# Weight and token sums issued ahead of their use, an output projection over eight banks, and transposes moved to other pairs

## The chip, the cores and the metric

The kernel runs on one core of a Trainium2 chip. That core has five engines, each with its own instruction queue that is worked off in order: TensorE (PE, matrix products), VectorE (DVE), ScalarE (ACT), GpSimd (POOL) and SyncE (SP, here the queue that issues the loads of weights). The metric is the device time of one execution in microseconds (us); the median of several executions is compared.

## The reference

One layer of a decoder trunk on 16 learned meta tokens and 256 tokens, width 2048, everything in float32. Three blocks add to the residual stream h:

```python
u = rms_norm(h, ffn1_norm_g[l])
h = h + 0.5 * swiglu(u, ffn1_w_gate[l], ffn1_w_up[l], ffn1_w_down[l])
...
z = u @ w_in[l]
q, k, v, qi, ki, wi, xc, gate_b, gate_c, ga, gc = jnp.split(z, SPLIT_POINTS, axis=-1)
...
merged = jax.nn.sigmoid(ga) * y_attn + jax.nn.sigmoid(gc) * y_conv
h = h + merged @ w_out[l]
...
h = h + 0.5 * swiglu(u, ffn2_w_gate[l], ffn2_w_up[l], ffn2_w_down[l])
return h[:, N_META:]
```

The change touches the second half: the two gates (ga and gc, each 2048 wide), the output projection w_out (2048 by 2048), and the second FFN (2048 to 5632 and back). The first FFN, the attention with its choice of 64 keys, and the short convolution stay as they are.

## The kernel before, in words

**Products in two parts.** A float32 product is made of three products of a faster 32-bit format: every operand is split into a high part (ACT copies it into that format) and a low part (DVE subtracts the copy from the original). High by high, high by low and low by high are added up in a PSUM bank. Weights are streamed, so each weight must be split when it comes: the class `Stream` does that.

**The stream.** A load (`load`, L126) brings 1 MB (128 x 2048) into one of three raw buffers, four in the second FFN. A load is cut into steps (`subs`) of at most 128 x 1024. `split` (L154) makes the high part (L175, tile `whi`) on ACT and the low part (L176, tile `wlo`) on DVE; there are four split buffers, six in the second FFN. Each time TensorE's program comes to a new step, `next` (L199) does, in this order: what was put down with `early`, the split of the step that lies three ahead (five in the second FFN), what was put down with `later` and is due, and then hands out the blocks. The lag given to `later` counts such calls: 1 is the next one. Since all engines take their instructions in the order in which they were written down, these calls set the order on ACT, DVE and POOL.

**Seven products instead of eight.** In the gates and the second FFN the work goes in groups. A group makes two blocks of 256 tokens by 512 columns (gate and up, or two column blocks of the down product) over pairs of 128 rows of the weights; a pair is one load. A pair of kind C takes the eight plain products (`plain_half`, twice, with a `hook(n)` between the halves). A pair of kind S takes seven products of sums, in Strassen's manner: sums of tokens (`sums_into`, L578, four subtractions and additions on POOL) against sums of weights. The weight sums are three DVE additions: `sumsa` (L143) and two for `sumsb` (L150, L151). An S load has four steps: "one" (128 x 512, raw), "sa" and "sb" (the sums) and "two" (raw). `total` writes down the additions of sa directly before the split of sa, and those of sb directly before the split of sb. The S pairs add into the banks q1, q5, q6, q7 besides q2 and q3 and q4, the C pairs into q2, q3, q4, q8. After the last S pair of a group `recombine` (L626) reads q1, q5, q6 and q7 into SBUF, which frees them; at the group's end `after_end` adds the rest.

**Order of the kinds.** In the gates, and in the first group of the second FFN, the order is `FIRST`, CCSCSCCC. In the other groups it is `KINDS`, SCCSCCCC; the last down group, with six pairs, has SCCCCC.

**Turns.** A gate column and an FFN group come out with tokens on the partitions; for the next product they are transposed on TensorE into two banks and split from there (`turn_four`, L596, with the copies at lags 1 and 2). `turn_merged` does it for the gates' result, `turn_mid` for the FFN's intermediate: for a group in the next up group at pair 5, for the last group of a part in the first half of the down group, at pair 5 of 8 or 3 of 6. The residual h is transposed in the first group of the second FFN (`turn_h`, eight turns, three banks, three to a pair from pair 5).

**Token sums.** `sums_of_tokens` (L586) scales two rows of h on ACT, sums on POOL, splits on ACT and DVE, all written down at once: for the gates twice, ahead of the first gate column (L1077), and for the second FFN inside the output projection (`made_of`, L1145).

**Output projection.** 16 tiles of 128 rows, each over 16 blocks (L1149 to L1163). The last four blocks come from the last gate column, which is still to be transposed, so four tiles take their first 12 blocks side by side in banks q2, q3, q4, q8, with loads of 12 and then of 4 blocks; the other 12 tiles follow in the same four banks by turns. After a tile, `add_to` (L375: DVE, ACT, DVE) adds it to h, and one call later `next_act2` and `square` make the next operands.

Of the kernel before, what the change touches and what calls it, by code (L numbers as in the profile page):

```python
# [9 lines left out]
F32 = mybir.dt.float32  # L10
# [5 lines left out]
P = 128  # L16
# [35 lines left out]
WIDE = 512  # L52
NG = FF // WIDE
PAIRS = KD // 2
KINDS = "SCCSCCCC"
ORDER = [2, 0, 1, 4, 3, 5, 6, 7]
PARTS = [range(0, 4), range(4, 8), range(8, NG)]
PLAN = [step for gs in PARTS for step in [("up", g) for g in gs] + [("down", gs)]]


FIRST = "CCSCSCCC"


def pairs_up(g):
# [16 lines left out]
class Stream:  # L81
# [7 lines left out]
    def __init__(self, nc, raw_pool, split_pool):  # L89
        self.nc = nc  # L90
        self.raw_pools, self.raw_bufs, self.n_raw = [raw_pool], RAW_BUFS, 0
        self.split_pools, self.ahead, self.n_tiles = [split_pool], AHEAD, 0
        self.sum_pool = None
        self.loads, self.subs = [], []
        self.raw, self.ready, self.sums = {}, {}, {}
        self.n_loaded = self.n_split = self.at = 0
        self.blocks, self.waiting, self.steps = [], [], []
        self.first = []
# [34 lines left out]
            self.raw[self.n_loaded] = raw  # L133
            self.n_loaded += 1

    def total(self, g, kind):

        raw = self.raw[g]
        name = f"sum{kind}"
        to = self.sum_pool.tile([P, 2 * WIDE], F32, name=name, tag=name)  # L140
        self.sums[g, kind] = to
        if kind == "sa":
            self.nc.vector.tensor_add(  # L143
                to.rearrange("p (q c) -> p q c", q=2),
                raw[:, WIDE : 3 * WIDE].rearrange("p (q c) -> p q c", q=2),
                raw[:, 3 * WIDE :].rearrange("p (q c) -> p q c", q=1).to_broadcast([P, 2, WIDE]),
            )
        else:
            sa = self.sums.pop((g, "sa"))
            self.nc.vector.tensor_add(to[:, :WIDE], sa[:, WIDE:], raw[:, WIDE : 2 * WIDE])  # L150
            self.nc.vector.tensor_add(to[:, WIDE:], to[:, :WIDE], raw[:, :WIDE])  # L151
        return to

    def split(self, upto):  # L154
        nc = self.nc
        while self.n_split < min(upto, len(self.subs)):
            if self.subs[self.n_split][1] == "sa" and not self.sum_pool:
                return
            g, kind, c, kk, width = self.subs[self.n_split]
            self.load(g + self.raw_bufs)  # L160
            n = kk * width
            if kind in ("sa", "sb"):
                raw = self.total(g, kind)
            elif kind == "two":
                raw = self.raw[g].rearrange("p (q c) -> p q c", c=WIDE)[:, 0:3:2, :]
            else:
                raw = self.raw[g][:, c : c + n]
            pool = self.split_pools[self.n_tiles % len(self.split_pools)]
            self.n_tiles += 1
            hi = pool.tile([P, SUB], F32R, name="whi")  # L170
            lo = pool.tile([P, SUB], F32R, name="wlo")
            to = [x[:, :n] for x in (hi, lo)]
            if kind == "two":
                to = [x.rearrange("p (q c) -> p q c", q=2) for x in to]
            nc.scalar.activation(to[0], raw, AF.Copy)  # L175
            nc.vector.tensor_sub(to[1], raw, to[0].bitcast(F32))  # L176
            self.ready[self.n_split] = [
                (hi[:, i * width : (i + 1) * width], lo[:, i * width : (i + 1) * width]) for i in range(kk)
            ]
            self.n_split += 1  # L180
            if kind == "sb":
                del self.sums[g, kind]
            if self.n_split == len(self.subs) or self.subs[self.n_split][0] > g:
                self.load(g + 1 + self.raw_bufs)

# [45 lines left out]
def tile_decoder_layer(  # L231
# [34 lines left out]
    def chunks(src, i0, i1, width=P):  # L266
        for i in range(i0, i1):
            st.add(src[i], RAW // width, width)
# [18 lines left out]
        for i in range(KC // 2):  # L287
            st.add(wb[c * KC // 2 + i], 4, WIDE)
    for a, b in ((0, 12), (12, KD)):
        for d in range(4):  # L290
            st.add(wo[d, :, a * P : b * P], b - a, P)
    chunks(wo, 4, KD)
    i = 0
    for kind, at in PLAN:
        for k in [p[0] for p in (pairs_up(at) if kind == "up" else pairs_down(at) * 2)]:
# [88 lines left out]
    def split_into(hi, lo, src):  # L384
        nc.scalar.activation(hi, src, AF.Copy)
        nc.vector.tensor_sub(lo, src, hi.bitcast(F32))
# [191 lines left out]
    def sums_into(t, x):  # L578

        t = t.rearrange("p (f t) -> p f t", f=4)  # L580
        nc.gpsimd.tensor_sub(t[:, 0, :], x[:, 0, :P], x[:, 0, P:])
        nc.gpsimd.tensor_sub(t[:, 1, :], x[:, 0, P:], x[:, 1, P:])
        nc.gpsimd.tensor_add(t[:, 2, :], x[:, 1, P:], t[:, 0, :])
        nc.gpsimd.tensor_sub(t[:, 3, :], x[:, 1, :P], t[:, 2, :])

    def sums_of_tokens(i, gain, to):  # L586

        x = small_tile("m0").rearrange("p (j t) -> p j t", j=2)
        t = small_tile("m1")
        for j in range(2):  # L590
            d = 2 * i + j
            nc.scalar.activation(x[:, j, :], h[:, d, META:], AF.Copy, scale=gain[:, d : d + 1])
        sums_into(t, x)
        split_into(to[:, 0, :], to[:, 1, :], t)

    def turn_four(to, m, tags, extra=None):  # L596

        for j in range(NT):
            ps = bank(tags[j], "pt")
            for f in range(4):  # L600
                nc.tensor.transpose(ps[:, f * P : (f + 1) * P], m[j][:, f * P : (f + 1) * P], ident)

            def after(j=j, ps=ps):
                cols = slice(j * P, (j + 1) * P)
                src = ps.rearrange("p (f t) -> p f t", f=4)
                for a, b, x in to:
                    split_into(x[:, :, 0, cols], x[:, :, 1, cols], src[:, a:b, :])
                if extra:
                    extra(src, cols)

            st.later(after, 1 + j)

    def group(todo, hook, after_seven, after_end):

# [36 lines left out]
    with ExitStack() as mix:  # L651
# [422 lines left out]

        act1 = act[:, :, :, LATER + META : LATER + T]
        made1 = {i: gp.tile([P, 2, 4 * P], F32R, name=f"made{i}") for i, k in enumerate(FIRST) if k == "S"}
        for i, to in made1.items():  # L1077
            sums_of_tokens(i, gains[1], to)

        ms, merged = {}, []  # L1080
        places = [[("tA", 4)], [("tB", 4)], [("zz0", 2), ("zz1", 2)], [("c0", 4)]]
# [64 lines left out]
            made[i] = spare[:, len(made)]  # L1146
            sums_of_tokens(i, gains[2], made[i])

        po = [bank(tag, "po") for tag in ("q2", "q3", "q4", "q8")]  # L1149
        for d in range(4):  # L1150
            paired(po[d], lambda k: ms[k], 0, 12, KD)
            if d == 1:
                turn_merged(("q1", "q5"))
        for d in range(KD):
            if d < 4:
                paired(po[d], lambda k: ms[k], 12, KD, KD)
            else:
                po.append(bank(("q2", "q3", "q4", "q8")[d % 4], "po"))
                paired(po[d], lambda k: ms[k], 0, KD, KD)
            st.later(lambda d=d: add_to(h[:, d, META:], po[d], 1.0, True))  # L1160
            st.later(lambda d=d: (next_act2(d), square(d, META)), 2)
            if d % 2 and FIRST[d // 2] == "S":
                st.later(lambda d=d: made_of(d // 2), 3)  # L1163
# [60 lines left out]
    def up_group(g):  # L1224

        def hook(n):
            if g == 0:
                if n == 0:
                    st.later(lambda: nc.vector.tensor_add(ssq[0][:, META:], ssq[0][:, META:], ssq[1][:, META:]))
                if n == 5:  # L1230
                    norm2()
                if n >= 5:
                    for i in range(3 * n - 15, min(3 * n - 12, 8)):
                        turn_h(i // 2, i % 2, ("q7", "q6", "q5")[i % 3])
            elif n == 5:
                turn_mid(("q1", "q5"))

        def after_end(q, buf):
            for tag in ("q3", "q2", "q4", "q8"):
                nc.vector.tensor_add(buf[tag], q[tag][0], buf[tag])  # L1240
            for j, tag in enumerate(("q2", "q3")):
                nc.scalar.activation(buf[tag], buf[tag], AF.Silu, scale=r2[:, 2 * j : 2 * j + 1])

            def products():
                m = [small_tile(f"m{j}") for j in range(NT)]
                for j, (u, s) in enumerate((("q4", "q2"), ("q8", "q3"))):
                    nc.vector.scalar_tensor_tensor(
                        m[j], buf[u], r2[:, 2 * j : 2 * j + 1], buf[s], op0=ALU.mult, op1=ALU.mult
                    )
                waiting.append((g, m))  # L1250

            st.later(products, 2)

        group(
            [(k, lambda i=i: four_of(act2, 2 * i, 2 * i + 1), lambda i=i: made[i]) for k, i in pairs_up(g)],
            hook, lambda buf: None, after_end,
        )

    PLACES = {"q2": (0, 0), "q3": (1, 0), "q4": (0, 1), "q8": (1, 1)}

    def down_group(gs, final):
        pairs = pairs_down(gs)
        for half in range(2):
# [13 lines left out]
            def after_end(q, buf, place=place):  # L1277
# [8 lines left out]
                    (k, lambda g=g, f=f: four_of(mids[g], f, f + 1), lambda g=g, f=f: made_mid[g, f])  # L1286
                    for k, g, f in pairs
                ],
                lambda n: n == len(pairs) - 3 and half == 0 and turn_mid(("q1", "q5")), after_seven, after_end,
            )  # L1290

    right = []
# [142 lines left out]
```

## Time and profile before

| | us |
|---|---|
| median of 3 runs | 2184.57 (2184.21 to 2185.79) |
| profiled execution, its own time | 2186.47 |
| span of the profiled execution, first to last instruction | 2184.7 |
| TensorE busy | 2149.4 |
| DVE busy | 1456.2 |
| ACT busy | 1035.0 |
| POOL busy | 60.4 |
| mean granted clock of TensorE | 0.997 |

Busy time is the time in which an engine had an instruction of the program at work. TensorE's pipelined matmuls overlap a little, and their ends are modelled. The view of waits gives, for an engine and a line, what it waited for in total, how often, and the longest. A timeline row gives the start, the time taken, the engine, the line, the operation with the tile written and the tiles read, the count, and in brackets the idle time before it and what ended that.

The stages in the profile: first FFN to about 800 us, projections, attention and convolution to 1086, the gates in four columns to 1353, the output projection to 1446, the second FFN to the end at 2184.7, with its down groups beginning near 1632, 1894 and 2112.

### The profile page before, as it was taken

Reading aid. Unit: us, or ns where it says so; the run is one execution under the profiler, and the core shown is the slowest. Engines: PE = TensorE matmul, PEld = TensorE weight load, DVE = VectorE, ACT = ScalarE, POOL = GpSimd, SP = SyncE. Lnnn points to the kernel's source line nnn. Section 1 sums busy time; section 2 is a strip of 40 time slices with the busy share of each in tenths; the row PEclk is TensorE's granted clock in tenths of the full one; section 3 lists DMA queues with packets and bytes.
Section 4 is the critical chain, followed back from the end, with each engine's and each line's share of the span. In section 5 each row is a group of like instructions: output and inputs, shape, how many; then the busy total and the mean of one; then the engine's idle time right before and its main releaser. Section 6 shows DMA issues by size and latency. Waiting matters only on the chain.

```text
span 2184.7 us, 31757 instructions
## 1 busy us (share of the span) xinstructions
PE 2149.4 (98%) x13102; PEld 1929.8 (88%) x13102; DVE 1456.2 (67%) x1823; ACT 1035.0 (47%) x1343; POOL 60.4 (3%) x82
## 2 busy tenths in 40 slices
PE   8999999999999999999999999999999999999998
PEld 8999999999999998898978888877887888878887
DVE  7555544455555555786567766678787878877785
ACT  6444433344444445564454444556554545444552
POOL 3000000000000000000000000110000000000000
PEclk9999999999999999999999999999999999999999
DMA  6555555555555545444455454555545554555453
GB/s 246 192 176 182 183 174 175 179 183 178 174 177 183 181 167 173 157 158 149 155 192 193 176 190 169 198 193 193 193 178 188 212 192 176 190 202 202 174 195 132
DMA packets 56881, 397.69 MB, mean 182 GB/s; under 512 B 6336, under 2 KB 6464, under 8 KB 9760
## 3 DMA queue, kind: packets, MB, share of 16 engines
q1 hardware_dynamic: 56448, 395.08, 50.9%
q8 instruction: 102, 1.67, 0.3%
q0 software_dynamic: 144, 0.42, 0.1%
q14 instruction: 43, 0.35, 0.0%
q10 hardware_dynamic: 144, 0.17, 0.0%
HBM read 393.54 MB, written 2.10 MB: 181 GB/s over the span
## 4 chain that ended last, share of the span: by engine, by line
PE 86%; DVE 8%; ACT 3%; issue 1%; POOL 1%; DMA 0%; SPq 0%; ACTq 0%; DVEq 0%
PE q L558 11%; PE q L557 11%; PE q L556 11%; DVE wlo L176 4%; PE pd L351 4%; PE pd L350 4%; PE pd L352 4%; PE pu L350 4%; PE pg L350 4%; PE pg L352 4%; PE pu L352 4%; PE pg L351 4%; PE pu L351 4%; ACT whi L175 3%; PE po L365 1%
## 5 line engine op out<-in xcount | busy, mean ns | idle before, releaser
L176 DVE TENSOR_TENSOR wlo<-raw,whi 128x1024 fp32r<-128x1024 f32 (+1 forms) x751 | 875.9, 1187 | 558.2 <-ACT whi L175 552.4
L175 ACT ACTIVATE whi<-raw 128x1024 fp32r<-128x1024 f32 (+1 forms) x751 | 757.7, 1026 | 752.8 <-PE q L558 146.1
L556 PE MATMUL q<-whi,act 128*128 128x512 f32 x898 | 352.0, 392 | 3.6 <-ACT u L381 2.3
L557 PE MATMUL q<-wlo,act 128*128 128x512 f32 x898 | 350.5, 390 | 2.3 <-DVE wlo L176 2.3
L558 PE MATMUL q<-whi,act 128*128 128x512 f32 x898 | 350.1, 390 | 0.0
L556 PEld LDWEIGHTS q<-whi,act 128*128 128x128 f32 x898 | 169.0, 188 | 39.9 <-ACT u L381 2.7
L557 PEld LDWEIGHTS q<-wlo,act 128*128 128x128 f32 x898 | 169.0, 188 | 37.9 <-DVE wlo L176 3.5
L350 PE MATMUL pd<-mid,whi 128*128 128x272 f32 x704 | 201.7, 286 | 0.0
L351 PE MATMUL pd<-mid,whi 128*128 128x272 f32 x704 | 201.7, 286 | 0.0
L352 PE MATMUL pd<-mid,wlo 128*128 128x272 f32 x704 | 201.7, 286 | 0.0
L558 PEld LDWEIGHTS q<-whi,act 128*128 128x128 f32 x898 | 169.0, 188 | 35.4
L350 PE MATMUL pg<-act,whi 128*128 128x272 f32 x672 | 192.7, 287 | 0.0
L352 PE MATMUL pg<-act,wlo 128*128 128x272 f32 x672 | 192.5, 287 | 0.0
L351 PE MATMUL pg<-act,whi 128*128 128x272 f32 x672 | 192.5, 287 | 0.0
L350 PE MATMUL pu<-act,whi 128*128 128x272 f32 x672 | 192.5, 286 | 0.0
L351 PE MATMUL pu<-act,whi 128*128 128x272 f32 x672 | 192.5, 286 | 0.0
L352 PE MATMUL pu<-act,wlo 128*128 128x272 f32 x672 | 192.5, 286 | 0.0
L350 PEld LDWEIGHTS pd<-mid,whi 128*128 128x128 f32 x704 | 132.6, 188 | 0.0
L351 PEld LDWEIGHTS pd<-mid,whi 128*128 128x128 f32 x704 | 132.6, 188 | 0.0
L352 PEld LDWEIGHTS pd<-mid,wlo 128*128 128x128 f32 x704 | 132.6, 188 | 0.0
L351 PEld LDWEIGHTS pg<-act,whi 128*128 128x128 f32 x672 | 126.6, 188 | 0.0
L350 PEld LDWEIGHTS pg<-act,whi 128*128 128x128 f32 x672 | 126.6, 188 | 0.0
(281 smaller groups left out, 3591.9 us busy)
## 6 DMA issues: line engine op xcount, KB each, us to landing
raw<-in_w_dram SPq DMA_DIRECT2D x132, 1024.0 KB, 4.9
raw<-in_wgu_dram SPq DMA_DIRECT2D x87, 1024.0 KB, 4.8
raw<-in_wd_dram SPq DMA_DIRECT2D x44, 1024.0 KB, 4.7
raw<-in_wg_dram SPq DMA_DIRECT2D x32, 1024.0 KB, 4.9
raw<-in_wcv_dram SPq DMA_DIRECT2D x24, 1024.0 KB, 4.8
raw<-in_wb_dram SPq DMA_DIRECT2D x16, 1024.0 KB, 4.9
raw<-in_wo_dram SPq DMA_DIRECT2D x12, 1024.0 KB, 4.9
raw<-in_wqi_dram SPq DMA_DIRECT2D x8, 1024.0 KB, 4.8
```

The costliest lines, as they stand in the source:

```text
L175: nc.scalar.activation(to[0], raw, AF.Copy)
L176: nc.vector.tensor_sub(to[1], raw, to[0].bitcast(F32))
L350: nc.tensor.matmul(ps, whi, xhi, start=first, stop=False)
L351: nc.tensor.matmul(ps, whi, xlo, start=False, stop=False)
L352: nc.tensor.matmul(ps, wlo, xhi, start=False, stop=last)
L365: nc.tensor.matmul(ps.rearrange("p (a t) -> p a t", a=2), whi, x(i), start=i == 0, stop=False)
L556: nc.tensor.matmul(ps, xhi, whi, start=n == 0, stop=False)
L557: nc.tensor.matmul(ps, xhi, wlo, start=False, stop=False)
L558: nc.tensor.matmul(ps, xlo, whi, start=False, stop=n == total - 1)
```

## The change: what it does

- `total` goes. `sum_ahead` writes down all three additions of an S load before the split of the step ahead of its first one ("one"), together with the load that this allows.
- `sums_of_tokens` puts its three parts down with `later`: scaling and POOL sums at lag `at` + 1, the split at lag `at` + 3. The gates' two calls are set three calls apart.
- `turn_four` puts both copies down at lag 1.
- `KINDS` becomes SCSCCCCC, with the order of the pairs to match. `turn_mid` comes one pair sooner in all places; the turns of h and the norm come one pair later, at pairs 6 (three turns) and 7 (five turns, over four banks).
- In the output projection five tiles stand side by side instead of four, and the tiles go through all eight banks; the turn of the last gate column uses q6 and q7 instead of q1 and q5.

```diff
-KINDS = "SCCSCCCC"
-ORDER = [2, 0, 1, 4, 3, 5, 6, 7]
+KINDS = "SCSCCCCC"
+ORDER = [2, 0, 4, 1, 3, 5, 6, 7]
...
+SIDE = 5
...
+    def sum_ahead(self):
+
+        for g, kind, _, _, _ in self.subs[self.n_split : self.n_split + 2]:
+            if kind in ("one", "sa") and self.sum_pool and g not in self.summed:
+                self.load(g + self.raw_bufs)
+                self.summed.add(g)
+                raw = self.raw[g]
+                sa, sb = (self.sum_pool.tile([P, 2 * WIDE], F32, name=f"s{i}", tag=f"s{i}") for i in "ab")
+                self.nc.vector.tensor_add(
+                    sa.rearrange("p (q c) -> p q c", q=2),
+                    raw[:, WIDE : 3 * WIDE].rearrange("p (q c) -> p q c", q=2),
+                    raw[:, 3 * WIDE :].rearrange("p (q c) -> p q c", q=1).to_broadcast([P, 2, WIDE]),
+                )
+                self.nc.vector.tensor_add(sb[:, :WIDE], sa[:, WIDE:], raw[:, WIDE : 2 * WIDE])
+                self.nc.vector.tensor_add(sb[:, WIDE:], sb[:, :WIDE], raw[:, :WIDE])
+                self.sums[g, "sa"], self.sums[g, "sb"] = sa, sb
...
                 return
+            self.sum_ahead()
             g, kind, c, kk, width = self.subs[self.n_split]
...
             if kind in ("sa", "sb"):
-                raw = self.total(g, kind)
+                raw = self.sums.pop((g, kind))
...
     for a, b in ((0, 12), (12, KD)):
-        for d in range(4):
+        for d in range(SIDE):
             st.add(wo[d, :, a * P : b * P], b - a, P)
-    chunks(wo, 4, KD)
+    chunks(wo, SIDE, KD)
...
-    def sums_of_tokens(i, gain, to):
+    def sums_of_tokens(i, gain, to, at=0):
...
-        for j in range(2):
+
+        def scaled(j):
             d = 2 * i + j
             nc.scalar.activation(x[:, j, :], h[:, d, META:], AF.Copy, scale=gain[:, d : d + 1])
-        sums_into(t, x)
-        split_into(to[:, 0, :], to[:, 1, :], t)
+
+        st.later(lambda: [scaled(j) for j in range(2)], at + 1)
+        st.later(lambda: sums_into(t, x), at + 1)
+        st.later(lambda: split_into(to[:, 0, :], to[:, 1, :], t), at + 3)
...
-            st.later(after, 1 + j)
+            st.later(after)
...
-        for i, to in made1.items():
-            sums_of_tokens(i, gains[1], to)
+        for n, (i, to) in enumerate(made1.items()):
+            sums_of_tokens(i, gains[1], to, 3 * n)
...
-        po = [bank(tag, "po") for tag in ("q2", "q3", "q4", "q8")]
-        for d in range(4):
+        tags = ("q2", "q3", "q4", "q8", "q1", "q5", "q6", "q7")
+        po = [bank(tags[d], "po") for d in range(SIDE)]
+        for d in range(SIDE):
             paired(po[d], lambda k: ms[k], 0, 12, KD)
             if d == 1:
-                turn_merged(("q1", "q5"))
+                turn_merged(("q6", "q7"))
         for d in range(KD):
-            if d < 4:
+            if d < SIDE:
                 paired(po[d], lambda k: ms[k], 12, KD, KD)
             else:
-                po.append(bank(("q2", "q3", "q4", "q8")[d % 4], "po"))
+                po.append(bank(tags[d % 8], "po"))
...
-                if n == 5:
+                if n == 6:
                     norm2()
-                if n >= 5:
-                    for i in range(3 * n - 15, min(3 * n - 12, 8)):
-                        turn_h(i // 2, i % 2, ("q7", "q6", "q5")[i % 3])
-            elif n == 5:
+                if n >= 6:
+                    for i in range(3) if n == 6 else range(3, 8):
+                        turn_h(i // 2, i % 2, ("q7", "q6", "q5", "q1")[(i - n + 6) % 4 if n > 6 else i])
+            elif n == 4:
                 turn_mid(("q1", "q5"))
...
-                lambda n: n == len(pairs) - 3 and half == 0 and turn_mid(("q1", "q5")), after_seven, after_end,
+                lambda n: n == len(pairs) - 4 and half == 0 and turn_mid(("q1", "q5")), after_seven, after_end,
```

More of the change, by code (lines that the diff above doesn't have):

```diff
@@ L94, in __init__ @@
         self.loads, self.subs = [], []
-        self.raw, self.ready, self.sums = {}, {}, {}
+        self.raw, self.ready, self.sums, self.summed = {}, {}, {}, set()
         self.n_loaded = self.n_split = self.at = 0
@@ L134, in load @@
             self.n_loaded += 1
[L136 to L152, printed above, removed]
+    def sum_ahead(self):
[13 more added lines that the diff above has]
+                self.sums[g, "sa"], self.sums[g, "sb"] = sa, sb
     def split(self, upto):
@@ L180, in split @@
             self.n_split += 1
-            if kind == "sb":
-                del self.sums[g, kind]
             if self.n_split == len(self.subs) or self.subs[self.n_split][0] > g:
```

## The prediction, made before the changed kernel was run

> **What bounds the kernel now.** I read the first lines of the page, then the waits of TensorE alone, then the same view in the stretch of each stage, and last the timelines of ScalarE (ACT) and VectorE (DVE) in front of each wait.
>
> ```profile
> span 2184.7 us, 31757 instructions
> PE 2149.4 (98%) x13102; PEld 1929.8 (88%) x13102; DVE 1456.2 (67%) x1823; ACT 1035.0 (47%) x1343; POOL 60.4 (3%) x82
> ...
> PE q L556 <- ACT mid L385: 5.9, 3, 2.3
> PE q L557 <- DVE wlo L176: 5.2, 9, 0.8
> PE q L556 <- ACT u L381: 2.3, 1, 2.3
> PE q L556 <- ACT whi L175: 2.3, 3, 1.0
> PE pht L1221 <- DVE vx L631: 2.3, 1, 2.3
> PE q L558 <- DVE mid L386: 1.4, 3, 0.6
> PE po L365 <- ACT whi L175: 1.4, 3, 0.9
> PE po L365 <- ACT u L381: 0.4, 1, 0.4
> PE pht L1221 <- DVE ve L633: 0.2, 1, 0.2
> ```
>
> Columns of the waits: us in total, times, longest. TensorE is busy for all but 35 us, and the change takes no matmul away. So it can win only these waits, which sum to 21.4 us, and what they cost in clock. By stage:
>
> ```profile
> PE q L557 <- DVE wlo L176: 2.7, 4, 0.8
> PE q L556 <- ACT whi L175: 2.1, 2, 1.0
> ...
> PE q L557 <- DVE wlo L176: 1.0, 3, 0.3
> ...
> PE q L557 <- DVE wlo L176: 1.5, 2, 0.8
> ```
>
> The stretches are the start of the gates (1085 to 1150), the other gates (1150 to 1350) and the entry to the second FFN (1446 to 1490). That places the 21.4: A, start of the gates 4.8; B, three later gate columns 1.0; C, output projection 1.8 (the two po rows); D, entry 4.0 (2.3 for u, 1.5, and 2.3 - 2.1 = 0.2 for whi); E, transposes of h 2.5 (the pht rows); F, the three down groups 7.3 (the mid rows).
>
> The clock costs more:
>
> ```profile
> 1485.00:1488.40 3.40, 3.40 (x11) 2.73 (x10) 2.51 (x4) 1.67 (x4) 0.00 (x0) 0.50 0.70 212
> 1488.40:1491.80 3.40, 3.40 (x16) 2.80 (x16) 0.99 (x1) 1.06 (x1) 0.00 (x0) 0.99 0.40 166
> 1669.30:1672.70 3.40, 3.40 (x10) 2.62 (x9) 0.73 (x2) 1.06 (x1) 0.00 (x0) 0.51 0.00 0
> 1928.75:1935.55 6.80, 6.28 (x14) 4.50 (x15) 3.50 (x5) 1.37 (x2) 0.00 (x0) 0.50 0.08 34
> ```
>
> The figure after the POOL column is the granted clock. It is half in three stretches, 13.6 us together, each right behind a wait of 2.3 us: E's, and F's first and second. Half clock costs at most 13.6 / 2 = 6.8. By the counts (16 matmuls in 3.4 us at full clock, so 5, 6 and 18 are missing, at 0.21 us, less 0.5 idle) it costs 5.7. I take 6.2: E 1.6, F 4.6. The third F wait, and D's 2.3 us, were followed by none.
>
> **A and B: sums ahead.** A weight tile of kind S needs 1215 + 683 + 714 ns = 2.6 us of sums, then low halves of 1224 ns:
>
> ```profile
> L143 DVE TENSOR_TENSOR sumsa<-raw 128x1024 f32<-128x1024 f32 x40 | 48.6, 1215 | 0.0
> L151 DVE TENSOR_TENSOR sumsb<-sumsb,raw 128x512 f32<-128x512 f32 x40 | 28.5, 714 | 1.4
> L150 DVE TENSOR_TENSOR sumsb<-sumsa,raw 128x512 f32<-128x512 f32 x40 | 27.3, 683 | 0.0
> L176 DVE TENSOR_TENSOR wlo<-raw,whi 128x1024 fp32r<-128x1024 f32 x699 | 842.5, 1224 | 543.1 <-ACT whi L175 541.2 <-PE po L365 0.5 <-PE q L558 0.5
> 1094.40 1.56 ACT L175 ACTIVATE whi<-raw 128x1024 fp32r<-128x1024 f32 x2
> 1098.53 1.06 ACT L175 ACTIVATE whi<-sumsa 128x1024 fp32r<-128x1024 f32 x1 [2.57 <-DVE sumsa L143]
> 1446.25 0.40 PE L556 MATMUL q<-whi,act 128*128 128x512 f32 x1
> 1449.45 0.39 PE L558 MATMUL q<-whi,act 128*128 128x512 f32 x1
> ```
>
> The last two rows are the first and last of 15 matmuls: 3.20 / 14 = 0.229 us each. So a half pair of kind C (12 matmuls) is 2.74 us, an S pair (21) 4.80. ACT waits 2.57 for a sum, while DVE idles 541 us in all ahead of low halves, for ACT. At the start of the gates all token sums, with a round trip over POOL, also stand before the first weight split at 1094.40. Now that split comes first, and the sums fill DVE's idle time. The same three additions run, none is saved.
>
> What they pass is the low half of the C half pair in front. Count from TensorE's start of a later gate column (0). DVE first has six operations of the merge, 6 x 0.68 = 4.1; sums to 6.7, that low half to 7.9; its matmul comes at 3 x 2.74 + 0.23 = 8.4. The second S: with four buffers the first S's last step can't be split before TensorE has left four half pairs, 10.9; split 1.06, two low halves 2.4: 14.4; sums 17.0, low half 18.2; its matmul comes at 4 x 2.74 + 4.80 + 2.74 + 0.23 = 18.7. Spare 0.5 each time. The same count with the old order has the second S's third low half at 23.8 against 23.5, a wait of 0.3, which is the row 1.0 over 3. In the first column DVE has one token split more (0.69), so 0.2 may stay. A wins 4.6, B 1.0. Both ends: if the spare is missed by its own size, 8 x 0.5 = 4 us come back; none can win more than its wait. The next load, now issued before the buffer's last reader, waits on SP for that reader as before; behind it on SP stand only later loads.
>
> In the second FFN six buffers run five steps ahead. At a group's start DVE does four additions (2.7), sums (2.6) and a low half (1.2), done at 6.5 against 4.80 + 2.74 + 0.23 = 7.8: nothing lost, 1.3 spare. S pairs at places 0 and 2 instead of 0 and 3 leave one C pair between them, which that count includes. That cover gone, an S pair costs up to its 2.6.
>
> **C: output projection.** Before, tile 4 waited for bank q2 (0.4); with eight banks no tile waits. The stall then goes to the backlog of additions behind the side-by-side tiles:
>
> ```profile
> 1374.91 1.23 DVE L176 TENSOR_TENSOR wlo<-raw,whi 128x1024 fp32r<-128x1024 f32 x1 [3.03 <-ACT whi L175]
> 1377.86 1.22 DVE L176 TENSOR_TENSOR wlo<-raw,whi 128x1024 fp32r<-128x1024 f32 x1 [0.52 <-ACT whi L175]
> 1381.22 1.23 DVE L176 TENSOR_TENSOR wlo<-raw,whi 128x1024 fp32r<-128x1024 f32 x1 [0.52 <-ACT whi L175]
> 1388.53 1.23 DVE L176 TENSOR_TENSOR wlo<-raw,whi 128x1024 fp32r<-128x1024 f32 x1 [0.52 <-ACT whi L175]
> 1393.41 1.23 DVE L176 TENSOR_TENSOR wlo<-raw,whi 128x1024 fp32r<-128x1024 f32 x1 [0.53 <-ACT whi L175]
> 1376.93 2.11 PE L365 MATMUL po<-ms,whi 128*128 128x512 f32 x8 [0.37 <-ACT u L381]
> ```
>
> A half tile is 8 matmuls of 512 columns and 8 of 256, 12 x 0.229 = 2.75 us. In the backlog DVE needs 3.4 a half tile (1377.86 to 1381.22), then 7.3 for two; afterwards 4.9 a whole tile (1388.53 to 1393.41) against 5.5. Before, DVE entered it 2.0 us ahead of TensorE (1374.91 against 1376.93). Five tiles side by side mean one addition more, one small load more on SP, one split more on ACT and DVE. The next tile's 1 MB load waits for the third load ahead of it, and between the two now lies a step of 1.4 where one of 2.75 lay: 1.4 later, so DVE enters 0.6 ahead. High halves are then ready at 2.8, 6.2, 10.1 and 13.8 (3.4, 3.9 and 3.7 apart), wanted at 2.75, 5.6, 9.0 and 12.9: 0.1 + 0.6 + 1.1 + 0.9 = 2.7 us. Against this the two waits behind the token sums go:
>
> ```profile
> 1400.55 1.32 POOL L581 TENSOR_TENSOR vm<-vm 128x128 f32<-128x128 f32 x1 [5.30 <-ACT vm L592]
> 1402.79 0.46 POOL L584 TENSOR_TENSOR vm<-vm,vm 128x128 f32<-128x128 f32 x1
> 1403.95 0.69 DVE L386 TENSOR_TENSOR act<-vm,act 128x512 fp32r<-128x512 f32 x1 [2.40 <-ACT act L385]
> ```
>
> DVE idled 2.40 there, twice; the split now comes two half tiles after the POOL work. Behind that on POOL stand only sums of squares, wanted in the next stage. POOL's four operations took 2.7, the first 1.32 while DVE worked, the last 0.46. Low end: no backlog stall, 0. High end: all four take 1.3, so 5.3, and 2.0 us of new waits. I take 2.7 for the projection, 0.9 worse than now. [...]
>
> **D: entry.**
>
> ```profile
> 1453.53 0.42 DVE L413 TENSOR_TENSOR ssq<-ssq,sq 128x256 f32<-128x256 f32 x1
> ```
>
> The last projection tile sat in q8, needed by the first pair: 2.3 us. Now the last four sit in q1, q5, q6, q7, which the first S needs 11 us later: gone. But DVE is free only at 1453.95, 7.7 after TensorE's start at 1446.25; sums and low half then end at 7.7 + 2.6 + 1.2 = 11.5, and the fourth half pair wants them at 8.4: a new wait of 3.0 in the place of the old. If DVE comes 4.8 earlier (both 2.40 stalls gone) it is nil. I take 1.8; the two S waits (1.5) and 0.2 go. D wins 2.2, so C and D together 1.3.
>
> **E and F: turns on other pairs.**
>
> ```profile
> 1482.56 0.69 DVE L631 TENSOR_TENSOR vx<-q,vv 128x512 f32<-128x512 f32 x1
> 1665.65 1.06 ACT L175 ACTIVATE whi<-sumsa 128x1024 fp32r<-128x1024 f32 x1 [3.99 <-DVE sumsa L143]
> 1666.62 0.58 ACT L385 ACTIVATE mid<-pt 128x512 fp32r<-128x512 f32 x1
> ```
>
> E: the turns wanted banks that DVE freed at 1483. One pair later is 5.5 us later: 2.5 and the clock's 1.6 won. Five turns now fall into one hook with four banks; the fifth waits for an ACT copy issued behind one split, 1.06 + 0.59 against 16 transposes, 1.8: about nil, 0.5 at most. F: the second copy (1666.62) stood behind a split that waited 3.99 for a sum. Now there is no such wait, both copies come in one step, and the turn comes one pair (5.5 us) sooner, against a lateness of 2.3 + 0.6. The tightest is the last down group, counted on DVE from its start: 4 additions 2.7, 4 low halves 4.9, 2 products 1.5, 4 recombinations 2.7, so bank q5 is free at 11.8, and the turn comes at 4.80 + 3 x 2.74 = 13.0; 4 additions 2.7, 4 low halves 4.9, 2 copies 1.4: 20.8, wanted at 4.80 + 6 x 2.74 = 21.2. F wins 7.3 and 4.6 of clock; low end: half a microsecond late three times.
>
> **The sum.** 4.6 + 1.0 + 1.3 + 2.5 + 7.3 + 6.2 = 22.9. The profiled execution took 2186.47, its span 2184.70 with 1.77 around it; 2163.6 of it is left. It lies 0.09% over the median of 2184.57, from which I count: 2161.7. Own range 2157 (all 27.6 won) to 2166.
>
> **Rivals.**
> 1. The projection and its handover lose more: POOL at 1.3 an operation (2.0), DVE as late at the entry as now (1.2), and a half-clock stretch behind that 3 us wait (1.6): 2166.5. For it: 1.32; against: DVE has idle time between its operations (0.52 before each row above).
> 2. The turns of F still come late, because DVE's queue (the last count leaves 0.4) reaches the copies late: F gives 4 of its 11.9, 2169.6; with rival 1 2174.
> 3. The clock drops don't hang on these waits. D's 2.3 us was followed by none. Then 6.2 stays: 2167.9. Against it: three drops, three waits directly ahead. [...] The rows show drops behind 2.3.
> 4. Slower: the sums in front of a low half, on DVE's queue, make it late at each of 40 S pairs. It decides from where DVE reaches the sums over 0.5 us (8 in the gates) or 1.3 us (32 in the FFN) later than counted. 2.0 us late costs 8 x 1.5 + 32 x 0.7 = 34.4: 2196.1. For it: the small spare; against: the 541 us of DVE's idle time ahead of low halves, where the sums go.
> 5. All waits gone: 2157.
>
> **Chances.** Forecast 0.52, rival 1 0.20, 2 0.10, 3 0.08, 4 0.05, 5 0.05. Under 0.2% (4.4 us) this kernel's time can't be told from no change. Faster: all but rival 4 and a part (0.04) of 2 that grows past 2180: 0.91. Same 0.05, slower 0.04. Range 2156.5 to 2174, up to rivals 1 and 2 together.
>
> **What would show it.** Right: ACT no longer waits for a weight sum; the rows q on mid, u and both pht rows are gone; granted clock 1.00 from 1480 to 1940. C: waits po on whi of 2 to 3 us, behind tile 5. D: one wait q on wlo at the fourth half pair. Wrong: new waits q on wlo at every S pair (rival 4), mid rows left over (2), half clock without a wait (3).

## The result and the profile after

The changed kernel takes 2159.32 us (median of four, 2158.81 to 2160.26), the kernel before beside it 2185.18 (2184.21 to 2187.13): 0.9881 of the time, 95% interval 0.9864 to 0.9898. The forecast was 2161.7, range 2156.5 to 2174. The profiled execution took 2160.26.

First lines of the page after, then TensorE's waits (us in total, times, longest):

```profile
span 2158.5 us, 31730 instructions
PE 2140.2 (99%) x13102; PEld 1929.4 (89%) x13102; DVE 1462.1 (68%) x1824; ACT 1043.2 (48%) x1344; POOL 72.6 (3%) x82
...
PE q L556 <- DVE wlo L177: 3.1, 2, 2.8
...
PE po L364 <- ACT whi L176: 1.4, 2, 0.7
```

The nine rows of before that the change could reach, 21.4 us in 25 waits, have become these two: 4.5 us in four. (The other rows, such as those of the first FFN, belong to stages that nothing was changed in.) Gone are both rows on `mid`, both on `pht`, and both of ACT's u. By the prediction's letters: A and B keep 0.3 us, C 1.4, E and F nothing. D has one wait of 2.8, at the fourth half pair as foretold, longer than foretold.

What ACT waited for, before (first two rows) and after (last two):

```profile
ACT whi L175 <- DVE sumsa L143: 100.2, 29, 4.3
ACT whi L175 <- DVE sumsb L151: 91.1, 36, 3.6
```

```profile
ACT whi L176 <- DVE sa L145: 9.2, 7, 1.7
...
ACT whi L176 <- DVE sb L150: 5.5, 3, 2.1
```

191 us of waiting for weight sums became 15. DVE's work is about the same (1462 us busy against 1456): the sums only stand elsewhere in its queue.

Windows behind two of the old waits on `mid` before, then the whole stretch from 1480 to 1940 after; the figure behind the POOL column is the granted clock, and it is 1.00 throughout:

```profile
1660.00:1680.00 20.00, 17.07 (x71) 13.22 (x70) 12.34 (x14) 5.84 (x7) 0.00 (x0) 0.91 0.36 130
1920.00:1945.00 25.00, 22.56 (x89) 17.58 (x88) 16.61 (x21) 8.59 (x10) 0.00 (x0) 0.86 0.34 127
```

```profile
1480.00:1940.00 460.00, 460.00 (x2072) 381.68 (x2072) 379.74 (x422) 246.38 (x281) 16.09 (x16) 1.00 0.55 196
```

And the new wait at D, in DVE's timeline (start, us, operation, in brackets the idle time before) and in two windows:

```profile
1446.33 0.42 DVE L412 TENSOR_TENSOR ssq<-ssq,sq 128x256 f32<-128x256 f32 x1
1446.66 1.22 DVE L145 TENSOR_TENSOR sa<-raw 128x1024 f32<-128x1024 f32 x1
...
1449.25 1.82 DVE L177 TENSOR_TENSOR wlo<-raw,whi 128x1024 fp32r<-128x1024 f32 x2
...
1447.30:1450.71 3.41, 0.59 (x2) 0.28 (x3) 3.34 (x5) 2.77 (x4) 0.00 (x0) 1.00 0.00 0
1450.71:1454.13 3.42, 3.42 (x9) 2.67 (x9) 3.42 (x5) 1.61 (x2) 0.00 (x0) 0.50 0.80 249
```

The second FFN began at 1438.80. DVE works off the tail of the projection until 1446.66, 7.9 us later, then does the three sums, and only at 1449.25 begins the low half that TensorE wants at 1447.7. The wait is followed by 3.4 us of half clock: 9 matmuls, where windows of this length at full clock held 16 or 17 (under the last heading). This execution has one more stretch of half clock, in the first FFN, that the change doesn't touch: 17.12 to 20.53, with 18 matmuls where the kernel before has 30 in as much time. The execution reaches the gates 1.1 us later (1087.24 against 1086.11). The sums below leave this stretch out unless they name it.

### The profile page after: what moved, and what is told of

Same layout as the page of the kernel before. It is cut to its first block, busy times and chain, and to the rows that moved or that the text cites. A ratio compares the mean times of both kernels' runs of the same rounds, so it can differ in the third digit from the quotient of the medians.

```text
span 2158.5 us, 31730 instructions
## 1 busy us (share of the span) xinstructions
PE 2140.2 (99%) x13102; PEld 1929.4 (89%) x13102; DVE 1462.1 (68%) x1824; ACT 1043.2 (48%) x1344; POOL 72.6 (3%) x82
## 4 chain that ended last, share of the span: by engine, by line
PE 94%; DVE 3%; ACT 2%; issue 1%; POOL 0%; DMA 0%; SPq 0%; ACTq 0%
PE q L556 13%; PE q L557 13%; PE q L555 13%; PE pd L351 4%; PE pd L350 4%; PE pd L349 4%; PE pu L349 4%; PE pg L349 4%; PE pu L350 4%; PE pg L350 4%; PE pg L351 4%; PE pu L351 4%; DVE wlo L177 1%; PE pbr L557 1%; PE pbr L555 1%; PE pbr L556 1%
## 5 line engine op out<-in xcount | busy, mean ns | idle before, releaser
L176 ACT ACTIVATE whi<-raw 128x1024 fp32r<-128x1024 f32 (+1 forms) x752 | 766.6, 1027 | 863.6 <-PE q L557 240.2
L350 PEld LDWEIGHTS pg<-act,whi 128*128 128x128 f32 x672 | 126.6, 188 | 0.0
L349 PEld LDWEIGHTS pu<-act,whi 128*128 128x128 f32 x672 | 126.6, 188 | 0.0
```

What stands on the lines that cost most here:

```text
L349: nc.tensor.matmul(ps, whi, xhi, start=first, stop=False)
L350: nc.tensor.matmul(ps, whi, xlo, start=False, stop=False)
```

## The experiments

Each figure is the median of four executions or more, taken beside the kernel before:

| kernel | us |
|---|---|
| before (its medians beside the experiments) | 2185.4 to 2186.6 |
| changed | 2159.3 |
| changed, weight sums in steps | 2185.6 |
| the same, and second S pair at its old place | 2195.0 |
| changed, turns of `mid` and S place as before | 2164.2 |
| the same, and second copy one step later | 2168.5 |
| changed, turns of h as before | 2159.3 |
| changed, token sums at once | 2167.0 |
| changed, second S pair at its old place | 2166.7 |
| changed, four tiles side by side | 2157.3 |
| four tiles, first sums of FFN2 later | 2155.3 |
| four tiles, first S pair of FFN2 later | 2153.8 |
| before, with the weight sums ahead alone | 2171.4 |
| before, with the early turn of `mid` alone | 2205.7 |

**Weight sums in steps.**

```diff
-            self.sum_ahead()
...
-                raw = self.sums.pop((g, kind))
+                raw = self.total(g, kind)
```

> The changed kernel with the weight sums of a kind S tile written where they stood before, each just ahead of the high half that reads it. My theory (each stage's waits went with the part of the change that I named for it): the start of the gates and the later gate columns lose again, 3 to 5 us of waits, ACT waits for weight sums again, some 190 us in all, but the turns of the middle tiles come one pair earlier with both copies in one step, so the matmuls on mid still wait for nothing: 2163 to 2167. Rival (the sums ahead of their use freed ACT, and that alone took away the waits on mid and the half clock behind them): these come back too, some 14 us, and the time is 2175 to 2180.

2185.58: ratio to before 0.9998 (0.9989 to 1.0007). All else of the change is in, and nothing is won. Neither theory had this size. TensorE's waits in that run, first of the whole, then from 1500 on:

```profile
PE q L558 <- DVE wlo L177: 12.1, 20, 0.8
...
PE q L557 <- ACT whi L176: 4.6, 11, 1.1
PE pht L1226 <- ACT ht L1227: 2.1, 1, 2.1
...
PE q L558 <- DVE wlo L177: 6.8, 9, 0.8
PE q L557 <- ACT whi L176: 2.5, 9, 0.3
```

The waits on `mid` stay away, as I had said, and against the rival. But nine later groups now lose 0.3 + 0.8 each at their second S pair; set against the changed kernel matmul by matmul, each costs 1.6 us, 14.6 in all (nine, not the eleven that the next expectation speaks of); 5.7 more are lost by the end of the projection, 4.8 at the entry. ACT waits for weight sums again, 212 us in all. Sums in steps and S pairs one C pair apart don't go together.

**The same, with the second S pair at its old place.**

```diff
-KINDS = "SCSCCCCC"
-ORDER = [2, 0, 4, 1, 3, 5, 6, 7]
+KINDS = "SCCSCCCC"
+ORDER = [2, 0, 1, 4, 3, 5, 6, 7]
```

> The changed kernel with the weight sums in steps, as in the first run, and the second kind S pair of a group back at place 3 instead of 2, nothing else. If what the first run lost in the second FFN (eleven times 1.6 us, one at each second S pair) comes from S pairs one C pair apart whose sums stand in steps: these eleven go, 2166 to 2171. If it comes from the sums alone: it stays, 2183 to 2187.

2194.98, ratio to before 1.0046 (1.0032 to 1.0060): slower than before, and outside both theories. The nine waits are gone, and ten others came:

```profile
PE pt L605 <- DVE ve L637: 18.3, 10, 1.9
```

The turn wants bank q5, which DVE's recombination still reads. With the S pair one later, the recombination is one pair later too, and an early turn runs into it. Three of the ten are followed by half clock; the mean granted clock of the execution was 0.997.

**The old place with the sums ahead.** The same diff, on the changed kernel.

> The changed kernel with the second kind S pair of a group back at place 3 instead of 2, nothing else; the turns stay one pair early. The run with the sums in steps and this place had ten waits of 1.9 us of the turns for a bank that the recombination still reads. If the place is what frees that bank in time: such waits come here too, 0.5 to 1.9 us at each of the turns, 2165 to 2181. If the sums ahead bring the recombination forward enough by themselves: no such wait, 2159 to 2160.

2166.7, in the range of "the place frees the bank". TensorE's waits from 1500 on, and the first of them in its timeline; last, the same place of the changed kernel:

```profile
PE pt L603 <- DVE ve L635: 5.5, 10, 0.5
...
1511.34 0.60 PE L603 MATMUL pt<-ident,vm 128*128 128x128 f32 x4
1512.49 0.66 PE L603 MATMUL pt<-ident,vm 128*128 128x128 f32 x4 [0.55 <-DVE ve L635]
1512.90 0.47 PE L555 MATMUL q<-whi,act 128*128 128x512 f32 x1
```

```profile
1513.30 1.03 PE L603 MATMUL pt<-ident,vm 128*128 128x128 f32 x8
1514.09 0.48 PE L555 MATMUL q<-whi,act 128*128 128x512 f32 x1
```

The sums ahead bring the recombination 1.4 us forward, the place of the S pair the rest. And the fence prices a wait: from the first turn to the next matmul 1.56 us against 0.79, so a wait shown as 0.55 costs 0.77. Ten make 7.7. The spans of the two profiled executions differ by 5.7 only, but the changed kernel's has 1.7 us lost to half clock behind D's wait and this one has none (mean granted clocks of 0.998 and 1.000): 5.7 + 1.7 = 7.4, or 8.5 with the 1.1 us lost in the first FFN. (The medians differ by 7.4 too, but this kernel's executions reach from 2166.0 to 2168.5.)

**The early turn alone, on the kernel before.**

```diff
-            elif n == 5:
+            elif n == 4:
                 turn_mid(("q1", "q5"))
...
-                lambda n: n == len(pairs) - 3 and half == 0 and turn_mid(("q1", "q5")), after_seven, after_end,
+                lambda n: n == len(pairs) - 4 and half == 0 and turn_mid(("q1", "q5")), after_seven, after_end,
```

> The kernel before with one part of the change alone: the turn of the middle tiles one pair earlier. Two things are asked. First, whether the part helps by itself: the waits on mid (7.3 us and 4.6 of clock) should go, but ten turns now meet a bank that VectorE still reads, 1.9 us each with some 0.3 beyond it, and some of these are followed by half clock: 2194 to 2204, slower. Rival (the turn gives its gain by itself): 2172 to 2175. Second, which waits cost clock. In the runs above the half-clock stretches begin on a grid of 3.413 us, and came behind waits of 1.94 to 2.8 us that lay inside one step of the grid, not behind as long waits that lay across two steps. If the clock follows the idle time of one step: of the ten waits here, those with 1.9 us or more inside one step are followed by half clock, those with less than 1.75 in each are not. If it follows the length of the wait: all ten, or none.

2205.7, ratio 1.0093 (1.0076 to 1.0110). The waits on `mid` are gone, yet by itself this part loses 19 us, a little more than I had said, because five of the ten waits for the bank are 2.7 rather than 1.9:

```profile
PE pt L601 <- DVE ve L633: 22.5, 10, 2.7
```

The clock's answer is under the last heading.

**The turns of `mid` and the S place as before.** Both edits above, undone in the changed kernel; in the second run also:

```diff
-            st.later(after)
+            st.later(after, 1 + j)
```

> The changed kernel with the turns of the middle tiles and the second kind S pair back where they were (hook 5 instead of 4, three pairs from the end instead of four, kind S at places 0 and 3); both copies stay in one step. If the earlier turn is what took the waits away: three waits on mid of 2 us each and two half-clock stretches come back, 2171 to 2174. If freeing ACT from its 4 us wait for a sum was enough (2.3 us late then, 4.0 won): no wait on mid, 2159 to 2161.

> As the run with the turns back, and the second copy of a turn one step later again, as before the change: what is left of the change in the down groups is the sums ahead alone. If these are enough: 2159 to 2163, no wait on mid over 1 us. If the place or the single step decides: 2171 to 2175, with half-clock stretches behind the waits on mid near 1670 and 1930.

2164.2 and 2168.5, between the two theories each time, so neither holds whole. The waits on `mid` in the first, then in the second:

```profile
PE q L557 <- DVE mid L385: 3.5, 3, 1.3
```

```profile
PE q L557 <- DVE mid L385: 5.8, 6, 1.3
```

Neither has half clock behind these (mean granted clock 0.999 in both, which is one stretch of 3.4 us). So of F's gain the sums ahead bring the shorter waits (the longest 1.3 us where it was 2.3) and with them the clock. By the medians, copying in one step brings 4.3 us and the early turn with the S place 4.9. By the profiled executions, each of which has one 3.4 us stretch of half clock behind D's wait, it is 2.9 and 4.0 (spans 2165.4, 2162.5, 2158.5), or 5.1 for the second without the 1.1 us that the changed kernel's lost in the first FFN. That fits the waits: 2.3 and 3.5 us of them go, three waits each time.

**The turns of h as before.**

```diff
-                if n == 6:
+                if n == 5:
                     norm2()
...
-                if n >= 6:
-                    for i in range(3) if n == 6 else range(3, 8):
-                        turn_h(i // 2, i % 2, ("q7", "q6", "q5", "q1")[(i - n + 6) % 4 if n > 6 else i])
+                if n >= 5:
+                    for i in range(3 * n - 15, min(3 * n - 12, 8)):
+                        turn_h(i // 2, i % 2, ("q7", "q6", "q5")[i % 3])
```

> The changed kernel with the turns of h and the sums over the second norm one pair earlier again, on three banks. My theory: the transposes wait for the banks that DVE reads in the recombination, 2.5 us, a stretch of half clock follows (1.6), and each wait costs some 0.27 more than its idle time: 2163 to 2165. Rival (that wait too came from DVE being late behind sums): no wait, 2159 to 2160.

2159.32, the rival's answer. TensorE's and DVE's timelines where the turns begin:

```profile
1474.13 1.51 PE L1224 MATMUL pht<-ident,h 128*128 128x128 f32 x12
...
1472.84 0.69 DVE L633 TENSOR_TENSOR vx<-q,vv 128x512 f32<-128x512 f32 x1
```

The turns don't wait. Before, the recombination's `vx` stood 36.3 us behind the stage's first matmul (1482.56 - 1446.25), here 33.8 (the stage starts at 1439.05). That the sums cured E is seen below too: with them alone no matmul on `pht` waits. The moved turns give nothing; with the sums in steps they even have their own wait, 2.1 us for an ACT copy (the `pht` row of the first run above).

**Token sums at once.**

```diff
-        st.later(lambda: [scaled(j) for j in range(2)], at + 1)
-        st.later(lambda: sums_into(t, x), at + 1)
-        st.later(lambda: split_into(to[:, 0, :], to[:, 1, :], t), at + 3)
+        for j in range(2):
+            scaled(j)
+        sums_into(t, x)
+        split_into(to[:, 0, :], to[:, 1, :], t)
```

> The changed kernel with the token sums of the gates and of the second FFN written at once again instead of in steps. Theory: at the start of the gates they stand ahead of the first weight split again, with ACT waiting for POOL: 2 to 4 us of waits there, and in the projection ACT and DVE wait 2.4 us for POOL twice, 1 to 2 us more: 2161 to 2165. If the sums ahead fill that time anyway: 2159 to 2160.

2166.95, more than I had expected: 7.6 us. DVE's queue at the start of the gates, and TensorE's waits from 1085 to 1150:

```profile
1094.87 0.69 DVE L385 TENSOR_TENSOR made<-vm,made 128x512 fp32r<-128x512 f32 x1 [2.68 <-ACT made L384]
1095.48 1.22 DVE L145 TENSOR_TENSOR sa<-raw 128x1024 f32<-128x1024 f32 x1
...
1098.07 1.82 DVE L177 TENSOR_TENSOR wlo<-raw,whi 128x1024 fp32r<-128x1024 f32 x2
...
PE q L556 <- DVE wlo L177: 3.0, 1, 3.0
```

Behind the late token split the sums ahead are harmful: they come in front of the first low half that TensorE wants, and make the wait 3.0 where it was 0.8, with 6.8 us of half clock behind it (mean granted clock of the execution 0.998). Set against the changed kernel matmul by matmul, this run loses 6.9 us at the start of the gates and 2.1 in the projection, and is 1.8 better at the entry, where D's wait has no half clock behind it.

**The sums ahead alone, on the kernel before.** `total` goes and `sum_ahead` comes, as in the change's diff, and nothing else.

> The kernel before with one part of the change alone: the weight sums ahead of their use. From the two runs above: without this part the rest gave nothing, and with the down groups' turns as before it left waits on mid of 1.1 and 0.8 three times. Theory now (this part carries most of the gain, the others take what is left in the down groups): half clock behind the waits on mid gone, no wait of the transposes of h, 2166 to 2172. Rival (no part gives anything by itself): 2182 to 2186.

2171.39, ratio 0.9933 (0.9918 to 0.9948): 15 of the 26 us. TensorE's waits, first of the whole, then from 1085 to 1150:

```profile
PE q L556 <- DVE mid L384: 5.8, 6, 1.3
...
PE q L555 <- DVE wlo L176: 3.0, 1, 3.0
```

It has the same 3.0 at the gates, D's old wait of 2.3 for u, and no wait on `pht`. That the wait for u went with the eight banks is read from this; no run has the eight banks alone.

**Four tiles side by side.** `SIDE = 4`.

> The changed kernel with four output tiles side by side instead of five, on the same eight banks. Theory from my count (each tile more side by side lets DVE enter the backlog later and adds one addition to it): the two waits of 0.7 behind tile 6 shrink to one of 0.5 at most, 2157.5 to 2159. Rival (the fifth tile covers the turn of the last merged column): a wait of the second part of tile 0 on ms appears, 2160 to 2162.

2157.27. The rival's wait on `ms` isn't there; TensorE's waits from 1370 on are two:

```profile
PE q L556 <- DVE wlo L177: 2.7, 1, 2.7
PE po L364 <- ACT whi L176: 0.4, 1, 0.4
```

The fifth tile costs 2 us (3.0 between the profiled spans, 2158.5 and 2155.5, with mean granted clocks of 0.998 and 0.999: both have one half-clock stretch at the entry, and 1.1 of the 3.0 is the changed kernel's other one) and buys nothing that these waits show.

**D: the first sums later, or the first S pair later.** Both on four tiles. First, the sums of the first S tile of the second FFN only when its high half needs them (`late` is that tile's load, `n` the step counted from the one being split):

```diff
-            if kind in ("one", "sa") and self.sum_pool and g not in self.summed:
+            if kind in ("one", "sa") and self.sum_pool and g not in self.summed and (g != self.late or n == 0 and kind == "sa"):
```

Second, another order of kinds in the first group:

```diff
+FIRST2 = "CCCSSCCC"
...
-ORDER = [2, 0, 4, 1, 3, 5, 6, 7]
+ORDER = [3, 0, 4, 1, 2, 5, 6, 7]
...
-    return list(zip(FIRST, range(PAIRS)) if g == 0 else zip(KINDS, ORDER))
+    return list(zip(FIRST2, range(PAIRS)) if g == 0 else zip(KINDS, ORDER))
```

> Four tiles side by side, and the sums of the first kind S tile of the second FFN written just ahead of the high half that reads them instead of two steps ahead (the other S tiles keep the look-ahead). Theory on the 2.7 us wait at the entry (VectorE reaches these sums 7.7 us late, and they push the low half of the fourth half pair): that low half comes 2.6 us sooner, the wait splits into some three of 0.4 to 0.9 us, no half clock follows: 2154 to 2155.5. Rival (the late tail of the projection alone makes it): the wait stays over 2 us, or moves whole to the S pair, with its half clock: 2157 to 2158.

> Four tiles side by side, and the first kind S pair of the second FFN one pair later (places 3 and 4 of the first group instead of 2 and 4). Theory: VectorE has 5.5 us more before the sums; left are 0.6 us at the fourth half pair and 0.3 at the second of the two S pairs that now stand side by side, no half clock: 2153 to 2154.5. Rival (two S pairs side by side starve TensorE, each second one by up to its 2.6 us of sums, and the first turns of h meet a late recombination): 2157 to 2160.

2155.27 (ratio 0.9862, 0.9845 to 0.9878) and 2153.75 (0.9856, 0.9841 to 0.9871). Waits from 1370 on, the first kernel, then the second:

```profile
PE q L559 <- DVE wlo L178: 1.8, 3, 0.7
PE po L367 <- ACT whi L177: 0.2, 1, 0.2
```

```profile
PE q L557 <- DVE wlo L178: 0.7, 1, 0.7
PE po L365 <- ACT whi L177: 0.3, 1, 0.3
```

Both theories held: the wait is DVE's lateness plus 2.6 us of sums, it splits or goes, and no half clock follows (mean granted clock 1.000 in both). The second kernel has the lowest median of all, 5.6 us under the changed one.

## Why the prediction was right, point by point

- **A and B** held: 4.8 became 0.3, 1.0 became none. A needs both steps, though; with the token sums at once TensorE leaves this stretch 0.8 us later than before the change.
- **C** was too dark. Step "1.4 later, so DVE enters 0.6 ahead": DVE entered it 1.5 ahead (the first two rows below), so two waits of 0.7 came and not four. POOL's four operations (the last rows):

```profile
1373.62 1.23 DVE L177 TENSOR_TENSOR wlo<-raw,whi 128x1024 fp32r<-128x1024 f32 x1 [1.85 <-ACT whi L176]
1375.09 2.00 PE L364 MATMUL po<-ms,whi 128*128 128x512 f32 x8
...
1398.40 1.11 POOL L580 TENSOR_TENSOR vm<-vm 128x128 f32<-128x128 f32 x1 [8.54 <-ACT vm L592]
1399.47 0.64 POOL L581 TENSOR_TENSOR vm<-vm 128x128 f32<-128x128 f32 x1
1400.08 0.46 POOL L582 TENSOR_TENSOR vm<-vm,vm 128x128 f32<-128x128 f32 x1
1400.61 1.35 POOL L583 TENSOR_TENSOR vm<-vm,vm 128x128 f32<-128x128 f32 x1
```

  They took 3.6 us, between my 2.7 and the high end of 5.3, and no matmul waited for it. Why two of them were slow, no run shows.
- **D** was too bright: the term "I take 1.8" was mis-sized. I let DVE come earlier because its two stalls shrink. They did, from 2.40 to 1.02 us each (the row below), but DVE came 7.9 us after the stage's start, as late as before. Why the time won did not reach the entry, no run separates. The end I had named for that case, 3.0, was right (2.82), and rival 1's half clock behind it came too, 1.7 us.

```profile
1402.66 0.69 DVE L385 TENSOR_TENSOR act<-vm,act 128x512 fp32r<-128x512 f32 x1 [1.02 <-ACT act L384]
```

- **E**: right size, wrong cause. "One pair later is 5.5 us later: 2.5 and the clock's 1.6 won" is the step that failed; the sums ahead by themselves let DVE free the banks in time.
- **F** held in size, and its three grounds (the freed ACT, the single step, the earlier pair) each carry a part. I had missed that the earlier pair is a loss unless the S pair moves and the sums come first.
- **What evened it out.** Waits shown went from 21.4 to 4.5, 16.9 less, and clock from 6.2 to 1.7, 4.5 less: together 21.4, under the forecast's 22.9. But the spans differ by 26.2. A wait cost more than the idle time shown, 0.22 us by the fence of the old place; 21 waits fewer make 4.6 us, an estimate from that one fence. The pages agree: for the same 13102 matmuls TensorE was busy 2149.4 us before and 2140.2 after, 9.2 less, and half clock accounts for 4.5 of it, or for 3.1 with the stretch in the first FFN (12 matmuls fewer, 0.114 us each). So does stage A, where 4.5 us of waits went and TensorE gained 6.1 us on the kernel before. That term was missing from the sum. It made up for what D lost and more, and that the total came out near the forecast is in part luck: C was put 1.3 us too dark, D 2.7 too bright, and some 4.7 was left out.
- **Rival 3** (clock apart from the waits) fell: the three old drops went with their waits, one came with D's and went with it again. **Rival 4** (sums in front of low halves) came true in one place of 40, at D. **Rival 2** (the turns come late) did not come; what late turns cost, the two runs that have them show: 4.9 and 9.2 us by the medians.

## What to carry to other kernels

Here moving 2.6 us of work ahead in an in-order queue paid where the queue had idled (ACT's 191 us of waiting became 15), and where the queue was already late it stood in waits of 2.8 us and, with the token sums at once, 3.0: look for the late places one by one (here the start of the gates and the entry to the second FFN), and leave the old order there. Parts of a change need not add up: the early turn alone lost 19 us and with the sums and the moved S pair won 4 to 5, so test a part both alone and taken out. And count waits, not only their sum: here each cost some 0.2 us beyond its idle time, by the estimate above.

## What the hardware showed

The half-clock stretches of these runs began on a grid of 3.413 us. In the kernel before they begin at 1485.03, 1669.35 and 1928.76, 54 and 76 steps of 3.4133 apart; in the changed kernel at 17.12 and 1450.72, 420 steps apart; in the run with the early turn alone, two of them at 1618.90 and 1666.69, 14 steps apart. They went with TensorE's idle time inside one step rather than with the length of a wait. By this reading it is no puzzle, as it was ahead of the prediction, that D's old wait of 2.3 us cost no clock while three others of 2.3 did: those had 1.91, 1.95 and 1.92 us idle inside one step (from 1481.62, 1665.94 and 1925.35). Windows on the grid around D's, the kernel before:

```profile
1447.48:1450.89 3.41, 2.35 (x11) 1.62 (x9) 2.38 (x4) 2.04 (x4) 0.89 (x1) 1.00 0.73 233
1450.89:1454.31 3.42, 2.16 (x9) 1.80 (x10) 1.98 (x5) 2.11 (x5) 0.11 (x1) 1.00 0.92 386
1454.31:1457.72 3.41, 3.41 (x16) 2.81 (x16) 2.96 (x3) 0.84 (x3) 0.00 (x0) 1.00 0.32 67
```

The wait lies across two steps, 1.1 and 1.3 us idle in each. The reading came from the earlier runs and was stated ahead of the run with the early turn alone. Four of its waits, each with the step behind it:

```profile
1567.70:1571.11 3.41, 1.93 (x11) 1.40 (x9) 3.34 (x5) 2.56 (x4) 0.00 (x0) 1.00 1.02 404
1571.11:1574.52 3.41, 2.15 (x12) 1.84 (x13) 3.41 (x5) 0.00 (x0) 0.00 (x0) 1.00 0.78 281
1574.52:1577.94 3.42, 3.42 (x17) 2.83 (x16) 1.63 (x3) 1.93 (x3) 0.00 (x0) 1.00 0.73 285
1615.49:1618.90 3.41, 0.69 (x7) 0.51 (x6) 3.34 (x6) 1.32 (x2) 0.00 (x0) 1.00 0.98 372
1618.90:1622.31 3.41, 3.41 (x11) 2.67 (x10) 2.31 (x3) 0.00 (x0) 0.00 (x0) 0.50 0.72 231
1663.27:1666.69 3.42, 1.47 (x10) 1.26 (x10) 3.39 (x6) 1.18 (x2) 0.00 (x0) 1.00 0.83 331
1666.69:1670.10 3.41, 3.41 (x10) 2.63 (x9) 3.41 (x5) 0.00 (x0) 0.00 (x0) 0.50 0.32 46
1792.98:1796.39 3.41, 1.49 (x9) 1.04 (x7) 3.34 (x6) 1.54 (x2) 0.00 (x0) 1.00 1.00 377
1796.39:1799.81 3.42, 3.39 (x17) 2.90 (x18) 2.84 (x3) 0.39 (x1) 0.00 (x0) 1.00 0.71 225
```

The first, 2.7 us split 1.5 and 1.3, costs no clock; the second and third, with 2.72 and 1.95 inside one step, do; the last, with 1.92, does not, against the reading. Of all ten, five were followed by half clock; with the old one at the turns of h these are six stretches, as the mean granted clock of 0.995 has it. In the changed kernel 1.80 was followed (13.70 to 17.11). So of the full-clock steps named here those with 1.5 us idle or less cost no clock, those with 1.95 or more did (1.95 twice, 2.72, 2.82), and from 1.80 to 1.92 both came: not sharp in this view. A step at half clock was followed by a second one with less, 0.51 us idle, in the kernel before (1928.76 to 1935.58). The same wait cost 0, 3.4 or 6.8 us at half clock by where it fell on the grid: D's 2.8 us did each of these, in the run with the S pair at its old place (1.49 and 1.39 us in two steps), in the changed kernel (2.82 in one step), and in the run with the turns of h as before (0.94 us idle in the 6.8). It seems to differ between executions of one kernel too: the last of these took 2157.8 and 2158.0 us at a mean granted clock of 1.000, and 2160.6 and 2161.5 at 0.998. A difference of 2 us between two medians may be this and no more.
